# First head's q half-strips stacked two value tiles later, their swaps bound behind value-tile stores in the transfer queue

## Chip, core and metric

The kernel runs on one core of one Trainium2 chip. The metric is the device time of one execution in microseconds (us). The kernel before took 1435.74 us (median of three runs, 1434.72 to 1436.17). The trace is of one profiled execution that took 1434.23 us, of which 1432.4 us lie between the first and the last instruction (the span). All times of day below are in us from the start of that span.

## What is computed

A two-layer encoder trunk on 1024 tokens of width 1024, in f32. Layer 0 is a differential attention, layer 1 a latent attention; only layer 0 matters here, and of it the start:

```python
def _diff_attention(h, positions, w_in, ...):
    proj = h @ w_in
    q, k, v, z = jnp.split(proj, [DA_WIDTH, 2 * DA_WIDTH, 3 * DA_WIDTH], axis=-1)
    q = _rope(q.reshape(b, s, 2 * DA_HEADS, DA_QK_DIM), positions)
    k = _rope(k.reshape(b, s, 2 * DA_HEADS, DA_QK_DIM), positions)
    ...
        sc = jnp.einsum('bqhcd,bkhcd->bhcqk', qb, k, preferred_element_type=f32) * scale
        p = jax.nn.softmax(sc, axis=-1)
        p = p[:, :, 0] - lam * p[:, :, 1]
        return jnp.einsum('bhqk,bkhd->bqhd', p.astype(v.dtype), v)
```

Each of 8 heads has two q and two k vectors of 64 per token (c = 0 and 1) and a value vector of 128. Beside this, every layer has shift, scale and gate vectors, each a product of a 1024-vector with a weight matrix (`_modulation`).

## The kernel before

Every f32 operand of a product is kept as two parts, high (rounded) and low (the rest), and a product is three matmuls (`mm3`, L186, L187, L188). Tokens come in two halves of 512 and in eight tiles of 128.

The engines work from queues that are filled at build time: a scheduler orders each engine's instructions, and an engine takes them strictly in that order. A transfer is issued by SP; an SP instruction that waits holds back every transfer behind it. Each SP transfer signals on one of eight semaphores in turn, and the ninth waits for the first. `tc.issue_after(ins)` adds one rule for the scheduler: what is traced inside the block comes after `ins` on the engine that `ins` is on.

The stretch that the change touches lies between 95 and 170 us, ahead of the attention loop of layer 0:

- **Value tiles.** The loop `for tt in range(8)` (L885) makes the values of heads 4 to 7 for eight token tiles, here called tile 0 to 7. `v0_tile` runs 24 matmuls into one PSUM bank (`vps`); `store_v` copies it out as a high part (ScalarE, L366, `v_hl<-vps`), subtracts for the low part (VectorE, the same line), and SP sends both to a scratch tensor in HBM (L368, `vS<-v_hl`, 512 KB). For tiles 0 to 5 the two-part tile `v_hl` has two buffers (`VB[0] = 2`): tile 2 needs the store of tile 0 to have landed, tile 3 that of tile 1, and so on. Tiles 6 and 7 (`V_LATE = 6`) take theirs from the buffers of the next item.
- **Modulation loads.** `next(mods_g)` loads 512 KB of a modulation weight (L423, `ada<-in_ada_ss` or `ada<-in_ada_g`) and lets VectorE reduce it (L444). The loop runs 13 of these (`MODS`), here called load 1 to 13, on three buffers: load 4 needs the reduction of load 1 to be done, and so on; tile 6 takes the buffer of load 11.
- **The first head's q and k.** Their projections were made before the loop. `rope` copies a half-strip out of PSUM, has SP swap its rows (L330), and multiplies; the closures left over for later are kept in the list `pend`: for each of k half 0, k half 1, q half 0 and q half 1 a rotation (GpSimd, L336) and a stacking. The four of k run before the loop. `stack_q` makes the two-part tiles `qa` and `qb` that the scores read: two ScalarE copies (L356, L357), two GpSimd subtractions (L358, L359), and four SP transfers of 128 KB inside SBUF (L361 and L362, the "swaps"), which copy each part into the other half of the partitions.
- **PSUM banks.** The accumulators of tiles 3 and 4 lie in the two banks that tiles 6 and 7 take again; so the first matmul of tile 6 waits for tile 3 to be copied out.
- **First scores.** At tile 6 the first head's first score tile is traced (`q_tile(0, 0, 0, ...)`, L873); the scheduler puts its matmuls near the end of tile 7. It reads `qa` and `qb` of q half 0. Row maximum (VectorE L404) and exponential (ScalarE L406) follow.

The code that places the stacking:

```python
    pend = [t for t in side.q if t]
    ...
        for t in pend[4 + 2 * tt : 6 + 2 * tt]:
            t()
        v0_tile(tt, 1, wv1)
```

Of the kernel before, what the change touches and what calls it, by code (L numbers as in the profile page):

```python
# [91 lines left out]
def trunk(ctx: ExitStack, tc: tile.TileContext, A, out):  # L92
# [22 lines left out]
    def psum(name, **tags):  # L115

        nonlocal ps, turn
        pst.close()
        NB.clear()
        NB.update(tags)  # L120
        turn = 0
        ps = pool(pst, name, bufs=1, space=PSUM)
# [642 lines left out]
    def v0_tile(tt, fh, wv):  # L765
        half, tl = tt // 4, tt % 4
        acc = bank("acc", "vps")
        c_ = slice(tl * P, (tl + 1) * P)
        for k in range(KT):
            hh, hl = h0[k][half]  # L770
            mm3(acc, hh[:, c_], hl[:, c_], wv[k][0], wv[k][1], k == 0, k == KT - 1)
        if tt < V_LATE:
            store_v(0, p1b, acc, tt, fh)
        else:
            store_v(0, pm, acc, tt, fh, "ada", 3)
# [80 lines left out]
    pend = [t for t in side.q if t]  # L856
# [6 lines left out]
    def q_tile(h, half, ti, zz, ep, mid=lambda i: None):  # L863

        ql = slice(ti * P, (ti + 1) * P)
        zs = [zz[:, ti : ti + 1], sm.tile([P, 1], F32, name="z1")]
        es = []
        qa, qb = QS[h][half]
        for c in range(2):
            s_ps = bank("sc", "s", [P, T])  # L870
            for src, fst in ((qa, True), (qb, False)):
                for kc in range(2):
                    PE.matmul(s_ps[:, kc * HF : (kc + 1) * HF], src[:, c, ql], KS[h][kc][:, c, :], start=fst, stop=not fst)  # L873
            with tc.issue_after(combined[-1]) if c == 0 and combined else nullcontext():
                es.append(softmax_part(None if c else ep, s_ps, zs[c], 1 if ep is a0a else 3))
            mid(c)
        e0, e1 = es
        z0, z1 = zs
        V.reciprocal(z1, z1)
        V.tensor_scalar(z1, z1, z0, neglam[:, 0:1], op0=ALU.mult, op1=ALU.mult)  # L880
        combined.append(V.scalar_tensor_tensor(out=e0, in0=e1, scalar=z1[:, 0:1], in1=e0, op0=ALU.mult, op1=ALU.add).ins)  # L881
        return e0

    first, combined = [], []
    for tt in range(8):  # L885
        if tt == V_LATE:
            psum("ps2", sc=2, tr=1, pv=1)
            zz0 = sm.tile([P, 4], F32, name="zz")
            first += [zz0, q_tile(0, 0, 0, zz0, a0a)]
        for _ in range(MODS[tt]):  # L890
            next(mods_g)
        for t in pend[4 + 2 * tt : 6 + 2 * tt]:
            t()
        v0_tile(tt, 1, wv1)
        if tt == HOLD:
            with tc.issue_after(store_v.last):
                for raw, src in held:
                    SP.dma_start(raw, src)
# [1046 lines left out]
```

## Time and profile before

| | before |
|---|---|
| median of 3 runs | 1435.74 us |
| profiled execution | 1434.23 us |
| its span | 1432.4 us |
| TensorE (PE) busy | 1399.6 us |
| VectorE (DVE) busy | 903.7 us |
| ScalarE (ACT) busy | 743.4 us |
| GpSimd (POOL) busy | 602.7 us |
| HBM and SBUF traffic | 201.64 MB, mean 141 GB/s |

PE is the engine that matters: a microsecond in which PE stands still, or runs at a lower clock, ahead of the attention loop is a microsecond that nothing later is known to hide. The other engines and the transfer queue count only where PE waits for them. "SPq" is SP's own queue: the time at which an instruction is issued there, not when its data lands. "PEclk" in a table of windows is the granted TensorE clock, 1.00 being full.

### The profile page before, as it was taken

What the parts mean: (1) busy time and instruction counts of PE and PEld (TensorE: products, weight loads), DVE (VectorE), ACT (ScalarE), POOL (GpSimd) and SP (SyncE); (2) the same over time, 40 slices, a digit from 0 to 9 for tenths busy, and PEclk for the clock granted to TensorE, in tenths of its full rate; (3) what the DMA queues carried; (4) which work ended last, traced back from release to release, by engine and by line L of the source; (5) the groups of instructions that cost most, each with busy time, mean ns of one, the idle gap of its engine ahead of it and who ended that gap; (6) DMA issues with size and microseconds to landing.
All of it is one profiled execution on the core that took longest, in us unless ns stands there. A gap on an engine that the chain in (4) does not pass through costs nothing.

```text
span 1432.4 us, 20749 instructions
## 1 busy us (share of the span) xinstructions
PE 1399.6 (98%) x7478; PEld 1169.8 (82%) x7478; DVE 903.7 (63%) x1366; ACT 743.4 (52%) x1318; POOL 602.7 (42%) x483
## 2 busy tenths in 40 slices
PE   9998999999999999998999999999999999999997
PEld 7786788888888887887888778887888888888886
DVE  7655687667777767677445877255566555555355
ACT  6622366656565656566443644345455554545442
POOL 4424164656564646453561244413241331412562
PEclk9999899999999999999999999999999999999999
DMA  9876723233333333336663232466343432336663
GB/s 355 263 232 199 242 66 103 82 104 84 99 84 96 88 97 82 104 85 225 216 224 117 61 104 88 140 182 180 110 117 114 132 100 77 103 96 213 218 209 138
DMA packets 128473, 201.64 MB, mean 141 GB/s; under 512 B 17777, under 2 KB 54769, under 8 KB 128370
## 3 DMA queue, kind: packets, MB, share of 16 engines
q1 hardware_dynamic: 128370, 200.31, 45.3%
q8 instruction: 59, 0.97, 0.3%
q14 instruction: 44, 0.36, 0.1%
HBM read 131.11 MB, written 45.55 MB: 123 GB/s over the span
## 4 chain that ended last, share of the span: by engine, by line
PE 84%; DMA 4%; DVE 4%; ACT 2%; POOL 2%; issue 2%; SPq 1%; POOLq 0%; ACTq 0%; DVEq 0%
PE s L1702 10%; PE acc L186 9%; PE acc L188 9%; PE acc L187 9%; PE tr L387 7%; PE s L873 7%; PE pv L187 4%; PE pv L188 4%; PE pv L186 4%; PE oacc L187 3%; PE oacc L188 3%; PE oacc L186 3%; PE zacc L186 1%; PE zacc L188 1%; PE zacc L187 1%
## 5 line engine op out<-in xcount | busy, mean ns | idle before, releaser
L389 ACT CAST pth<-tr 128x512 fp32r<-128x512 f32 x256 | 150.3, 587 | 279.8 <-PE tr L387 276.8
L404 DVE TENSOR_REDUCE nm<-s 128x1 f32<-128x1024 f32 x192 | 233.9, 1219 | 76.5 <-PE s L873 70.1
L390 DVE TENSOR_TENSOR ptl<-tr,pth 128x512 fp32r<-128x512 f32 x256 | 176.1, 688 | 136.6 <-ACT pth L389 136.1
L235 POOL TENSOR_TENSOR wl<-wraw,wh 128x512 fp32r<-128x512 f32 (+2 forms) x82 | 101.4, 1239 | 232.2 <-ACT wh L234 204.7
L387 PE MATMUL tr<-ident,e 128*128 128x128 f32 x1024 | 154.7, 273 | 4.1 <-DVE ptl L390 3.9
L406 ACT ACTIVATE e<-s,nm 128x1024 f32<-128x1024 f32 x128 | 143.5, 1121 | 28.9 <-DVE nm L404 28.5
L387 PEld LDWEIGHTS tr<-ident,e 128*128 128x128 f32 x1024 | 120.8, 140 | 45.9 <-DVE ptl L390 22.5
L186 PE MATMUL acc<-h0h,wh 128*128 128x512 f32 x360 | 151.0, 419 | 1.7 <-DVE v_hl L366 1.7
L186 PE MATMUL pv<-pth,vt 128*128 128x256 f32 x512 | 147.3, 288 | 0.0
L187 PE MATMUL pv<-ptl,vt 128*128 128x256 f32 x512 | 145.8, 285 | 0.0
L188 PE MATMUL pv<-pth,vt 128*128 128x256 f32 x512 | 144.6, 282 | 0.0
L188 PE MATMUL acc<-h0h,wl 128*128 128x512 f32 x360 | 142.9, 397 | 0.0
L187 PE MATMUL acc<-h0l,wh 128*128 128x512 f32 x360 | 142.0, 395 | 0.0
L1117 POOL TENSOR_TENSOR wol<-wor,woh 128x512 fp32r<-128x512 f32 x64 | 85.0, 1348 | 84.2 <-ACT woh L1116 84.0
L186 PEld LDWEIGHTS pv<-pth,vt 128*128 128x128 f32 x512 | 97.3, 190 | 3.2 <-ACT pth L389 0.8
L187 PEld LDWEIGHTS pv<-ptl,vt 128*128 128x128 f32 x512 | 97.4, 190 | 2.8
L188 PEld LDWEIGHTS pv<-pth,vt 128*128 128x128 f32 x512 | 97.7, 191 | 0.1
L873 PE MATMUL s<-ks,qa 128*128 128x512 f32 x256 | 82.8, 404 | 3.5 <-DVE e L881 2.7
L331 POOL TENSOR_TENSOR rp_r<-rp_raw,cosT 128x512 f32<-128x512 f32 x38 | 49.6, 1306 | 85.4 <-ACT rp_raw L326 52.1
L336 POOL TENSOR_TENSOR rp_sw<-rp_sw,sinT 128x512 f32<-128x512 f32 x42 | 55.6, 1324 | 71.1 <-DMA rp_sw<-rp_raw 70.9
L881 DVE SCALAR_TENSOR_TENSOR e<-s,z,e 128x1024 f32<-128x1024 f32 x64 | 82.1, 1283 | 2.1
L873 PE MATMUL s<-ks,qb 128*128 128x512 f32 x256 | 81.0, 396 | 0.4 <-DMA qb<-qb 0.4
(624 smaller groups left out, 3359.4 us busy)
## 6 DMA issues: line engine op xcount, KB each, us to landing
ada<-in_ada_ss SPq DMA_DIRECT2D x32, 512.0 KB, 6.7
wraw<-in_w_s SPq DMA_DIRECT2D x64, 256.0 KB, 2.8
vS<-v_hl SPq DMA_DIRECT2D x32, 512.0 KB, 4.8
vt<-vS SPq DMA_DIRECT2D x32, 512.0 KB, 4.6
wor<-in_w_out SPq DMA_DIRECT2D x64, 256.0 KB, 3.5
rp_sw<-rp_raw SPq DMA_DIRECT2D x168, 64.0 KB, 2.0
bc_s<-bc_d SPq DMA_DIRECT2D x30, 256.0 KB, 4.3
oS<-bc_s SPq DMA_DIRECT2D x30, 256.0 KB, 2.6
```

The lines of the kernel that those rows point to most:

```text
L186: PE.matmul(psum, ah, bh, start=first, stop=False)
L187: PE.matmul(psum, ah, bl, start=False, stop=False)
L188: return PE.matmul(psum, al, bh, start=False, stop=last).ins
L235: sub = (lo_on or (V if pair_of else G)).tensor_sub(l_[:, :n], raw[:, :n], f32v(h_[:, :n]))
L387: PE.transpose(tr[:, j, :], p[:, kt * P : (kt + 1) * P], ident)
L389: mk["S"] = S.copy(pth[kh][:, :, dst], tr).ins
L390: mk["V"] = V.tensor_sub(ptl[kh][:, :, dst], tr, f32v(pth[kh][:, :, dst])).ins
L404: mk["V"] = V.reduce_max(nm, s_ps, axis=AX.X, negate=True).ins
L406: mk["S"] = S.activation(e, s_ps, AF.Exp, bias=nm, scale=1.0, accum_out=zs).ins
L873: PE.matmul(s_ps[:, kc * HF : (kc + 1) * HF], src[:, c, ql], KS[h][kc][:, c, :], start=fst, stop=not fst)
L1117: in_turn(G.tensor_sub(lo, raw, f32v(hi)))
L1702: PE.matmul(s_ps[:, kc * HF : (kc + 1) * HF], lhs, rhs(kc), start=i == 0, stop=i == 4)
```

## The change

```diff
@@ -889,8 +889,9 @@
             first += [zz0, q_tile(0, 0, 0, zz0, a0a)]
         for _ in range(MODS[tt]):
             next(mods_g)
-        for t in pend[4 + 2 * tt : 6 + 2 * tt]:
-            t()
+        for t in pend[2 * tt : 2 + 2 * tt] if tt > 1 else ():
+            with tc.issue_after(store_v.last):
+                t()
         v0_tile(tt, 1, wv1)
         if tt == HOLD:
             with tc.issue_after(store_v.last):
```

q half 0 is now rotated and stacked in the round of tile 2 instead of tile 0, and q half 1 in that of tile 3 instead of tile 1. Whatever these closures issue on SP comes behind the store that was traced last at that point: the store of tile 1 for half 0 and that of tile 2 for half 1. Nothing is added or removed. All lines of the file from L894 on move down by one.

On SP, before, from the store of tile 0 (first row; `vS_1_70` is the scratch tensor of heads 4 to 7) to the store of tile 1 (last row):

```order
L368 DMA vS_1_70<-v_hl 256x4x128
L361 DMA qa<-qa 64x512
L362 DMA qa<-qa 64x512
L361 DMA qb<-qb 64x512
L362 DMA qb<-qb 64x512
L423 DMA ada<-in_ada_ss 128x1024 x2
L361 DMA qa<-qa 64x512
L362 DMA qa<-qa 64x512
L361 DMA qb<-qb 64x512
L362 DMA qb<-qb 64x512
L368 DMA vS_1_70<-v_hl 256x4x128
```

All eight swaps stand between the two stores, and loads 3 and 4 between the two sets of swaps. On SP, now, from the store of tile 0 to the store of tile 2:

```order
L368 DMA vS_1_70<-v_hl 256x4x128
L423 DMA ada<-in_ada_ss 128x1024 x2
L368 DMA vS_1_70<-v_hl 256x4x128
L423 DMA ada<-in_ada_ss 128x1024
L423 DMA ada<-in_ada_g 128x1024
L361 DMA qa<-qa 64x512
L362 DMA qa<-qa 64x512
L361 DMA qb<-qb 64x512
L362 DMA qb<-qb 64x512
L368 DMA vS_1_70<-v_hl 256x4x128
```

Only loads 3 and 4 are left between the stores of tiles 0 and 1; the swaps of half 0 stand behind loads 5 and 6 and ahead of the store of tile 2. Then follow, now:

```order
L423 DMA ada<-in_ada_g 128x1024 x2
L361 DMA qa<-qa 64x512
L362 DMA qa<-qa 64x512
L361 DMA qb<-qb 64x512
L362 DMA qb<-qb 64x512
L368 DMA vS_1_70<-v_hl 256x4x128
L423 DMA ada<-in_ada_g 128x1024 x3
```

The swaps of half 1 stand behind loads 7 and 8 and ahead of the store of tile 3; from there on SP's order is as it was.

On PE one matmul of tile 7 changes sides with the first score tile. This piece of the difference is at the end of tile 7 (`vps` is the tile's accumulator, `s` the scores):

```order
 L186 MATMUL vps<-wvh,h0h_1_128 128x512
-L873 MATMUL s<-ks,qa 128x512 x2
-L873 MATMUL s<-ks,qb 128x512 x2
-L873 MATMUL s<-ks,qa 128x512 x2
-L873 MATMUL s<-ks,qb 128x512 x2
 L187 MATMUL vps<-wvl,h0h_1_128 128x512
+L873 MATMUL s<-ks,qa 128x512 x2
+L873 MATMUL s<-ks,qb 128x512 x2
+L873 MATMUL s<-ks,qa 128x512 x2
+L873 MATMUL s<-ks,qb 128x512 x2
 L188 MATMUL vps<-wvh,h0l_1_129 128x512
```

The scores come one matmul later. The orders of VectorE, ScalarE and GpSimd are the same before and now.

## The prediction

> **What bounds the kernel now.** I began with the page: busy times, and the chain that ended last.
>
> ```profile
> PE 1399.6 (98%) x7478; PEld 1169.8 (82%) x7478; DVE 903.7 (63%) x1366; ACT 743.4 (52%) x1318; POOL 602.7 (42%) x483
> PE 84%; DMA 4%; DVE 4%; ACT 2%; POOL 2%; issue 2%; SPq 1%; POOLq 0%; ACTq 0%; DVEq 0%
> ```
>
> PE sets the end, so a change of transfer order is worth what PE stands still or runs slowly for it. I therefore asked for the waits between 95 and 175 us (total, count, longest):
>
> ```profile
> ACT v_hl L366 <- DMA vS<-v_hl: 20.5, 2, 16.5
> PE vps L186 <- DVE v_hl L366: 5.3, 1, 5.3
> PE acc L186 <- DVE v_hl L366: 1.7, 1, 1.7
> ```
>
> One PE wait of 5.3 us stands in a value tile, and one ScalarE wait of 16.5 us for a store. PE's timeline shows what it costs (start, duration, bracket: idle before):
>
> ```profile
> 135.83 0.39 PE L188 MATMUL vps<-wvh,h0l 128*128 128x512 f32 x1
> 141.49 0.79 PE L186 MATMUL vps<-wvh,h0h 128*128 128x512 f32 x1 [5.27 <-DVE v_hl L366]
> 142.09 0.63 PE L187 MATMUL vps<-wvl,h0h 128*128 128x512 f32 x1
> ...
> 146.35 0.63 PE L188 MATMUL vps<-wvh,h0l 128*128 128x512 f32 x1
> ...
> 147.14 0.39 PE L187 MATMUL vps<-wvl,h0h 128*128 128x512 f32 x1
> ...
> 153.49 0.39 PE L188 MATMUL vps<-wvh,h0l 128*128 128x512 f32 x1
> 153.72 0.39 PE L186 MATMUL vps<-wvh,h0h 128*128 128x512 f32 x1
> 153.95 0.62 PE L873 MATMUL s<-ks,qa 128*128 128x512 f32 x2
> ```
>
> Tile 6 starts at 141.49. At the full step (147.14 to 153.72 in 29 steps, 0.227 us) it would have started at 136.06, so the stall is 5.43 us. Then matmuls step at 0.426 us (142.09 to 146.35 in ten steps) until 146.8. From 141.49 to the first scores at 153.95 stand 43 matmuls, 12.46 us where 43 x 0.227 = 9.76 would do: 2.70 us more. Stall and slow clock are **8.13 us**.
>
> Why PE waited is in the queues of ScalarE and VectorE, which copy tile 3 out:
>
> ```profile
> 140.13 0.58 ACT L366 CAST v_hl<-vps 128x512 fp32r<-128x512 f32 x1 [16.49 <-DMA vS<-v_hl]
> 140.75 0.69 DVE L366 TENSOR_TENSOR v_hl<-vps,v_hl 128x512 fp32r<-128x512 f32 x1 [2.24 <-ACT v_hl L366]
> ```
>
> The copy waits 16.49 us for a store to land. SP's own queue (start and duration of the issue) says which:
>
> ```profile
> 112.13 0.66 SPq L368 DMA_DIRECT2D vS<-v_hl  x1
> 120.60 0.53 SPq L361 DMA_DIRECT2D qa<-qa  x1
> ...
> 129.98 0.46 SPq L362 DMA_DIRECT2D qb<-qb  x1
> 130.53 1.02 SPq L423 DMA_DIRECT2D ada<-in_ada_ss  x2
> 131.65 0.47 SPq L361 DMA_DIRECT2D qa<-qa  x1
> ...
> 134.08 0.73 SPq L368 DMA_DIRECT2D vS<-v_hl  x1
> ...
> 143.11 0.59 SPq L368 DMA_DIRECT2D vS<-v_hl  x1
> ```
>
> The copy of tile 3 needs the buffer of tile 1, whose store SP issues at 134.08, behind eight swaps and loads 3 and 4. The swaps wait for their own operands on GpSimd; meanwhile the transfer engines carry next to nothing (windows: PE, PEld, DVE, ACT, POOL busy, granted clock, DMA share, GB/s):
>
> ```profile
> 120.00:130.00 10.00, 10.00 (x46) 8.26 (x45) 7.25 (x9) 3.54 (x7) 9.72 (x6) 1.00 0.18 41
> 132.00:156.00 24.00, 18.73 (x71) 14.95 (x70) 11.98 (x19) 1.76 (x3) 0.67 (x1) 0.86 1.01 325
> 136.00:138.00 2.00, 0.22 (x1) 0.00 (x0) 0.85 (x3) 0.00 (x0) 0.00 (x0) 1.00 1.07 253
> 141.49:146.78 5.29, 5.29 (x13) 4.13 (x13) 4.24 (x7) 0.58 (x1) 0.00 (x0) 0.50 1.06 343
> 160.50:164.50 4.00, 4.00 (x11) 3.18 (x12) 4.00 (x8) 1.17 (x3) 0.00 (x0) 0.57 0.86 282
> ```
>
> 41 GB/s over ten microseconds, then 325 GB/s for 24: the load is pushed together.
>
> **The change, part by part.** Nothing is computed more or less; PE, VectorE, ScalarE and GpSimd keep their instructions, and all but PE their order. The terms:
>
> *Store of tile 1.* Behind load 4 now, which takes load 1's buffer (VectorE's timeline; the first row is the last reduction of the loads before these 13):
>
> ```profile
> 111.22 1.28 DVE L444 CUSTOM_DVE_ANT_0 ada<-ada,c,vec 128x1024 f32<-128x1024 f32 x1
> ...
> 114.51 0.69 DVE L366 TENSOR_TENSOR v_hl<-vps,v_hl 128x512 fp32r<-128x512 f32 x1 [2.00 <-ACT v_hl L366]
> ...
> 122.87 2.33 DVE L444 CUSTOM_DVE_ANT_0 ada<-ada,c,vec 128x1024 f32<-128x1024 f32 x1
> ...
> 127.36 0.68 DVE L366 TENSOR_TENSOR v_hl<-vps,v_hl 128x512 fp32r<-128x512 f32 x1
> ```
>
> and the time from issue to landing of all 32 stores:
>
> ```profile
> DMA to landing us min/median/max: 3.5/4.8/7.6
> ```
>
> Tile 1's data is ready at 115.20. Load 1's reduction ends at 125.20, so load 4 goes out there and the store at about 125.8 (0.5 us per issue, half of the 1.02 row). By the row's ends it lands between 129.3 and 133.4. Copy, subtraction and PE's start took 141.49 - 140.13 = 1.36 us, so tile 3 is out by 134.8 at the worst, ahead of 136.06. Neither end of the landing costs anything: the 5.43 us go, and I let the 2.70 go with them, since PE then has no idle time ahead of tile 6.
>
> *Store of tile 2, swaps of half 0.* The low parts come from GpSimd:
>
> ```profile
> 128.66 1.29 POOL L359 TENSOR_TENSOR qb<-rp_r,qa 64x512 fp32r<-64x512 f32 x1
> 131.38 1.29 POOL L359 TENSOR_TENSOR qb<-rp_r,qa 64x512 fp32r<-64x512 f32 x1
> ```
>
> Half 0 is ready at 129.95. Loads 5 and 6 ahead of it wait for the reductions of loads 2 and 3, about 127.4 and 129.3 (tile 2's subtraction ends at 128.04, one reduction more). Four swaps take 134.08 - 131.65 = 2.43 us of SP, so the store goes out at about 132.4 and lands by 140.0; tile 4 is out by 141.4, and tile 7 wants its bank at 136.06 + 24 x 0.227 = 141.51. Just in time at the worst end. The swaps are out by 132.4 too, 13 us before the scores read them.
>
> *Store of tile 3, swaps of half 1.* Ready on GpSimd at 132.67; load 8 ahead waits for load 5's reduction, about 134 (it follows tile 3's subtraction and its own landing). Store 3 goes out at about 136.6 instead of 143.11.
>
> *One matmul ahead of the scores.* They begin at 136.06 + 44 x 0.227 = 146.05, which is **7.90 us** earlier; the matmul itself costs PE nothing, but the chain that follows runs through the scores, so 8.13 - 0.23 counts.
>
> *What is late next.* Behind the scores comes VectorE, in an order that stays:
>
> ```profile
> 150.00 1.28 DVE L444 CUSTOM_DVE_ANT_0 ada<-ada,c,vec 128x1024 f32<-128x1024 f32 x1
> 155.07 1.23 DVE L404 TENSOR_REDUCE nm<-s 128x1 f32<-128x1024 f32 x1 [3.78 <-PE s L873]
> ...
> 157.41 1.28 DVE L444 CUSTOM_DVE_ANT_0 ada<-ada,c,vec 128x1024 f32<-128x1024 f32 x1
> ...
> 159.75 0.69 DVE L366 TENSOR_TENSOR v_hl<-vps,v_hl 128x512 fp32r<-128x512 f32 x1
> ```
>
> The first maximum stands behind load 9's reduction (150.00), load 11's (157.41) ahead of the copy of tile 6, for which PE waits 1.7 us. All this should move 7.90 us up, to a maximum at 147.17 and load 11's reduction at 149.51, if the transfers keep up. Loads 4 to 11, stores 1 to 3 and eight swaps are 8 x 0.524 + 3 x 0.524 + 8 x 0.131 = 6.81 MB. At 325 GB/s these are 21.0 us; counted from 126.6 (load 4's issue and an estimated 1.4 us until data flows, as from 130.53 to the crowded window's 132.00) they end at 147.6, 1.9 us early. At 253 GB/s, the thinnest crowded window, they take 26.9 us and end at 153.5, 4.0 us late. So this term costs 0 to 4.0; I take 0.6, close to the 24 us row, for holes where a load waits for a reduction or for one of the eight semaphores (a third of one load's 0.524 MB / 325 GB/s = 1.6 us).
>
> **Sum:** 7.90 - 0.6 = 7.3 us. Against the profiled execution, 1434.23, this gives 1426.9; that execution lay 1.51 us below the median, so for the median **1428.4 us**. A measurement of this kernel tells about 0.2%, 2.9 us, from no change.
>
> *A rule weighed.* The row 141.49:146.78 shows a granted clock of 0.50 for 5.29 us after the stall. The Trainium skill ("TensorE: Matmul & The Clock Gate", Part 1) says that PE falls to half rate after an idle window of about 3.4 us and comes back after some 3.4 us of work; by it the slow stretch would be worth an estimated 1.7 instead of 2.70 us (3.4 us at half rate), and the forecast 6.3. The trace shows longer, and the trace decides.
>
> **Rivals.** *The second slow stretch goes as well.* After the 1.7 us wait at `acc` the clock is 0.57 until 164.5: 4.00 x (1 - 0.57) = 1.7 us. For it: nearly the same wait elsewhere costs no clock if PE's idle time happens to be spread. Against: the chain that makes the wait stays. Then 9.0 us, 1426.7. By the same part of the skill's page an idle time this short should leave the clock alone; the row 160.50:164.50 disagrees.
>
> *Transfers bind.* Below 6.81 MB / (149.51 - 126.6) = 297 GB/s load 11 is late and its lateness is PE's. At 253 GB/s the gain is 3.9 us, 1431.8. For it: share 1.01 over 24 us. Against: bytes that waited now use the empty stretch.
>
> *The change doesn't free the store.* Load 3, which I let go right behind the store of tile 0, was never seen free: SP stood in the swaps. If its buffer, or load 4's, is held to about 134, store 1 leaves as late as before: 1435.7. Against: VectorE is through with the older loads at 111.22 + 1.28 = 112.5, and load 1's reduction stands at 122.87 whatever SP does.
>
> *Slower: the store of tile 3 is now the held one.* It stands behind the four swaps of half 1 and loads 7 and 8. The first maximum cannot start before its landing plus copy 0.62, subtraction 0.69 and load 9's reduction 1.28. If it lands after 155.07 - 2.6 = 152.5, everything behind is later than before; 3 us past that give 1438.7. For it: the same kind of wait held store 1 for 19 us. Against: its operands are on GpSimd by 132.67, 15 us earlier than needed.
>
> **Chances.** Forecast 0.56, second slow stretch gone 0.12, transfers bind 0.14, store not freed 0.11, slower 0.07. Faster by over 0.2%: 0.82; within: 0.11; slower: 0.07. The range takes in the first three: from 1426.7 less the runs' spread downwards, 1425.4, to 1431.8 and half a microsecond of spread, 1432.6.
>
> **What would show it.** Right: store 1 issued near 126, no PE wait ahead of tile 6, clock 1.00 from 120 to 148, first scores near 146, the 41 GB/s stretch filled from 125 on. Wrong: a wait of ScalarE's copy for a store beyond 136, of VectorE's maximum for load 9, or PE's wait at `acc` well over 1.7 us; and a gain at 146 that later stages lose again.

## The result, and the profile after

| | before | with the change |
|---|---|---|
| median, first comparison (6 runs each) | 1436.34 us | 1431.15 us, ratio 0.9963 [0.9950, 0.9976] |
| median, second comparison (25 and 6 runs) | 1433.66 us | 1428.06 us, ratio 0.9959 [0.9945, 0.9974] |
| profiled execution (its span) | 1434.23 (1432.4) us | 1429.47 (1427.7) us |
| PE busy | 1399.6 us | 1396.7 us |

The change makes the kernel faster, by 5.2 and 5.6 us in the two comparisons; 7.3 us were forecast. Both intervals lie wholly below 0.998, so this is more than the 0.2% that a measurement of this kernel can mistake.

The page of the kernel with the change, the busy times and the chain that ended last:

```profile
PE 1396.7 (98%) x7478; PEld 1167.8 (82%) x7478; DVE 903.3 (63%) x1366; ACT 743.3 (52%) x1318; POOL 603.7 (42%) x483
PE 80%; DVE 6%; DMA 5%; issue 3%; ACT 3%; POOL 2%; SPq 1%; ACTq 0%; POOLq 0%; DVEq 0%
```

PE has as many instructions as before and 2.9 us less of busy time (matmuls at a lower clock count as longer). That this is near the 2.70 us of the slow stretch that is gone is partly chance: in a second trace of each kernel, 1398.8 and 1398.6 us, PE's busy time differs by 0.2 us only; the step from 6.3 us to the medians, below, gives part of the reason. PE still sets the end.

The waits between 95 and 175 us, the three rows that answer to those shown of before:

```profile
ACT v_hl L366 <- DMA vS<-v_hl: 21.3, 3, 8.8
...
PE s L873 <- ACT e L406: 2.1, 1, 2.1
PE acc L186 <- DVE v_hl L366: 1.7, 1, 1.7
```

The row of 5.3 us, PE's wait ahead of tile 6, is gone. ScalarE waits for stores as long as before in sum, but in three pieces of at most 8.8 us instead of two of up to 16.5, and none of these pieces reaches PE's value tiles. PE's wait for the exponential of the first scores has grown from 0.5 to 2.1 us; it is taken up below, at what is late next.

SP's own queue (start and duration of the issue):

```profile
114.05 0.66 SPq L368 DMA_DIRECT2D vS<-v_hl  x1
114.81 13.21 SPq L423 DMA_DIRECT2D ada<-in_ada_ss  x2
128.11 0.64 SPq L368 DMA_DIRECT2D vS<-v_hl  x1
...
135.31 0.63 SPq L368 DMA_DIRECT2D vS<-v_hl  x1
136.03 2.28 SPq L423 DMA_DIRECT2D ada<-in_ada_g  x2
138.96 0.47 SPq L361 DMA_DIRECT2D qa<-qa  x1
...
141.46 0.63 SPq L368 DMA_DIRECT2D vS<-v_hl  x1
142.19 5.37 SPq L423 DMA_DIRECT2D ada<-in_ada_g  x3
```

Only loads 3 and 4 stand between the stores of tiles 0 and 1. ScalarE's copies of tiles 1, 3 and 5 (bracket: idle before, and for what):

```profile
116.35 0.59 ACT L366 CAST v_hl<-vps 128x512 fp32r<-128x512 f32 x1 [7.33 <-PE vps L188]
...
134.86 0.58 ACT L366 CAST v_hl<-vps 128x512 fp32r<-128x512 f32 x1 [8.76 <-DMA vS<-v_hl]
...
148.60 0.59 ACT L366 CAST v_hl<-vps 128x512 fp32r<-128x512 f32 x1 [5.90 <-DMA vS<-v_hl]
```

**How to compare two traces here.** The copy of tile 1 lies ahead of everything that the change moves, and yet it starts at 113.89 us in the trace of before and at 116.35 in this one, at 114.72 in a second trace of the changed kernel and at 115.46 in a second trace of the kernel before. What lies ahead of it varies by more than some terms of the sum. So the times of day below are also given from the start of that copy, written "T1 + ...". Store 1 goes out at T1 + 20.2 before (134.08 - 113.89) and at T1 + 11.76 now (128.11 - 116.35). In two traces of each kernel, four points on the path (`acc` is a projection behind the first scores, `pv` the first product with the values):

| trace | T1 | first scores | first maximum | first `acc` matmul | first `pv` matmul |
|---|---|---|---|---|---|
| before | 113.89 | T1 + 40.06 | T1 + 41.18 | T1 + 46.61 | T1 + 65.36 |
| before, second trace | 115.46 | 39.65 | 40.77 | 46.19 | 64.82 |
| with the change | 116.35 | 32.19 | 34.77 | 40.18 | 58.91 |
| with the change, second trace | 114.72 | 32.18 | 34.57 | 39.98 | 59.85 |

On the means, the scores start 7.7 us earlier (39.86 to 32.19), the first row maximum 6.3 (40.98 to 34.67), the first matmul of `acc` 6.3 (46.40 to 40.08), the first product with the values 5.7 (65.09 to 59.38). So 1.4 us are lost between the scores and the maximum. PE's rows show where they appear:

```profile
148.54 0.62 PE L873 MATMUL s<-ks,qa 128*128 128x512 f32 x2
...
153.63 0.72 PE L873 MATMUL s<-ks,qa 128*128 128x512 f32 x2 [2.15 <-ACT e L406]
...
156.53 0.75 PE L186 MATMUL acc<-h0h,wh 128*128 128x512 f32 x1 [1.73 <-DVE v_hl L366]
```

and VectorE's rows between them why:

```profile
149.22 0.69 DVE L366 TENSOR_TENSOR v_hl<-vps,v_hl 128x512 fp32r<-128x512 f32 x1 [2.02 <-ACT v_hl L366]
149.90 1.28 DVE L444 CUSTOM_DVE_ANT_0 ada<-ada,c,vec 128x1024 f32<-128x1024 f32 x1
...
151.12 1.22 DVE L404 TENSOR_REDUCE nm<-s 128x1 f32<-128x1024 f32 x1
```

The scores start at 148.54, the maximum over them at 151.12, 2.58 us later (1.12 before). VectorE goes without a break from tile 5's subtraction to load 9's reduction to the maximum, and the subtraction waits for tile 5's copy, which waits for store 3 to land. The value tiles no longer wait for a store; the maximum now does.

Windows of the changed kernel (PE, PEld, DVE, ACT, POOL busy, granted clock, DMA share, GB/s):

```profile
122.00:132.00 10.00, 9.93 (x44) 8.19 (x45) 9.22 (x11) 4.00 (x8) 9.73 (x6) 1.00 0.37 103
134.00:151.50 17.50, 17.48 (x77) 14.09 (x75) 9.85 (x17) 1.76 (x3) 2.79 (x2) 1.00 1.02 311
156.50:162.00 5.50, 5.47 (x17) 4.39 (x18) 5.48 (x9) 1.20 (x3) 0.00 (x0) 0.69 0.84 272
```

The clock is full up to the scores. After the two waits it is 0.69 for 5.50 us in this trace, a loss of 5.50 x 0.31 = 1.7 us, the same as before; in the second trace of the changed kernel it is lower and costs more (below). And the transfers are as crowded as before: 1.02 of the engines' time at 311 GB/s.

### The profile page after: what moved, and what is told of

It reads as the page before. It is cut to its first block, busy times and chain, and to the rows that moved or that the text cites. A ratio compares the mean times of both kernels' runs of the same rounds, so it can differ in the third digit from the quotient of the medians.

```text
span 1427.7 us, 20748 instructions
## 1 busy us (share of the span) xinstructions
PE 1396.7 (98%) x7478; PEld 1167.8 (82%) x7478; DVE 903.3 (63%) x1366; ACT 743.3 (52%) x1318; POOL 603.7 (42%) x483
## 3 DMA queue, kind: packets, MB, share of 16 engines
HBM read 131.11 MB, written 45.55 MB: 124 GB/s over the span
## 4 chain that ended last, share of the span: by engine, by line
PE 80%; DVE 6%; DMA 5%; issue 3%; ACT 3%; POOL 2%; SPq 1%; ACTq 0%; POOLq 0%; DVEq 0%
PE s L1703 9%; PE acc L188 8%; PE acc L186 8%; PE acc L187 8%; PE tr L387 7%; PE s L873 7%; PE oacc L186 4%; PE oacc L188 4%; PE oacc L187 4%; PE pv L187 4%; PE pv L188 4%; PE pv L186 4%; DVE ada L444 2%; PE zacc L186 1%; PE zacc L188 1%
## 5 line engine op out<-in xcount | busy, mean ns | idle before, releaser
L390 DVE TENSOR_TENSOR ptl<-tr,pth 128x512 fp32r<-128x512 f32 x256 | 176.1, 688 | 136.6 <-ACT pth L389 136.1
```

What stands on the lines that cost most here:

```text
L390: mk["V"] = V.tensor_sub(ptl[kh][:, :, dst], tr, f32v(pth[kh][:, :, dst])).ins
```

## The experiments

Every kernel computes the whole reference. Three theories are named by letters in what was expected. **Q**, the queue: what counts is only the order on SP, that is, when stores 1 and 2 go out. **P**, the place of the arithmetic: what counts is where the rotation and stacking stand in the program, and what the scheduler makes of it. **D**, the transfers: behind the scores the engines that carry the data are full, and what is left to gain goes with the bytes ahead of store 3. Ratios are against runs of the kernel before on the same chip, with their 95% intervals.

**The change again** (`after_again`), no edit.

> Theory Q (queue): the gain is that SP lets the store of tile 1 out about 8 us earlier; what is missing of the forecast 7.3 us is a later store of tile 3 (1.5 us where 0.6 was forecast) and chance ahead of the change. Then the profile shows the copy of tile 1 to the store of tile 1 in about 11.8 us, first scores 32.2 us behind the copy of tile 1, and the time is 5.0 to 7.0 us below before. If the 2.5 us by which the copy of tile 1 stood later in the first profile (116.35 instead of 113.89) are chance, it stands near 114 to 115 now; if they belong to this build, near 116.3 again. Rival D (transfers bind): the gain is what the transfer engines allow, under 4 us.

Measured: 1428.06 against 1433.66 us, 0.9959 [0.9945, 0.9974]. Its trace has store 1 at T1 + 11.76, to the hundredth as in the first; no wait ahead of tile 6; the maximum 2.39 us behind the scores. The gain and the loss behind the scores are both properties of the kernel; T1, at 114.72 instead of 116.35, is not.

**Only the swaps moved** (`swaps_only`). In the kernel before, rotation and stacking stay in rounds 0 and 1; only the swaps are kept back, and traced behind the stores of tiles 1 and 2.

```diff
-        for t in (qa, qb):
-            SP.dma_start(f32v(t[64:128, 0, :]), f32v(t[0:64, 0, :]))
-            SP.dma_start(f32v(t[0:64, 1, :]), f32v(t[64:128, 1, :]))
+        def swap():
+            for t in (qa, qb):
+                SP.dma_start(f32v(t[64:128, 0, :]), f32v(t[0:64, 0, :]))
+                SP.dma_start(f32v(t[0:64, 1, :]), f32v(t[64:128, 1, :]))
...
+        if tt in (1, 2):
+            with tc.issue_after(store_v.last):
+                held_swaps.pop(0)()
```

> The stacking is traced where it was before; only the eight swaps are taken out of it and issued behind the stores of tile 1 (half 0) and tile 2 (half 1). Theory Q (SP's order is all of the change): the stores of tile 1 goes out 11.8 us behind the copy of tile 1, PE has no wait ahead of tile 6, and from the copy of tile 1 to the first matmul at acc it takes 40 to 41 us (before 46.6, the change 40.2 and 40.0); the time is that of the change within 1 us. Rival P (the place of the stacking's arithmetic matters): the gain is clearly smaller than the change's, 3 us or less.

SP's queue of this kernel (its lines are numbered 8 higher, so that the stores are L376 and the loads L431):

```profile
114.08 12.69 SPq L431 DMA_DIRECT2D ada<-in_ada_ss  x2
126.87 0.64 SPq L376 DMA_DIRECT2D vS<-v_hl  x1
...
133.72 0.64 SPq L376 DMA_DIRECT2D vS<-v_hl  x1
```

T1 is 115.09, so store 1 leaves at T1 + 11.78, as with the change. Measured: 1428.53 against 1434.02 us, 0.9964 [0.9950, 0.9977]; `acc` starts at T1 + 40.81. This is the change's gain without moving a line of the arithmetic. Q holds, P falls.

**Only half 1 moved** (`half1_only`). Half 0 stays in the round of tile 0, half 1 goes to that of tile 3.

```diff
-        for t in pend[2 * tt : 2 + 2 * tt] if tt > 1 else ():
-            with tc.issue_after(store_v.last):
+        for t in {0: pend[4:6], 3: pend[6:8]}.get(tt, ()):
+            with tc.issue_after(store_v.last) if tt > 1 else nullcontext():
```

> Half 0's stacking and swaps as before, half 1's as in the change. The store of tile 1 then stands behind four swaps (last operand ready 16.1 us behind the copy of tile 1) and loads 3 and 4: it goes out about 17.7 us behind that copy (before 20.2, the change 11.8). Theory Q: tile 3 comes out some 2.2 us earlier than before, PE's wait ahead of tile 6 shrinks from 5.3 to 3 or 3.5 us and does not vanish; from the copy of tile 1 to acc about 44 us with the slow clock still behind the wait, 42 without; time 2 to 4.5 us below before. Rival D (transfers bind): the gain does not follow the store of tile 1, and is as large as the change's or none.

SP's queue and, below it, PE at the start of tile 6:

```profile
131.41 0.46 SPq L362 DMA_DIRECT2D qb<-qb  x1
131.96 1.02 SPq L423 DMA_DIRECT2D ada<-in_ada_ss  x2
133.04 0.64 SPq L368 DMA_DIRECT2D vS<-v_hl  x1
```

```profile
140.90 0.80 PE L186 MATMUL vps<-wvh,h0h 128*128 128x512 f32 x1 [3.23 <-DVE v_hl L366]
```

With four swaps still ahead of it, store 1 leaves at T1 + 17.71 (T1 is 115.33) and PE waits 3.23 us, with the slow clock behind it (0.52 in the window from 141 to 147). Measured: 1431.57 against 1434.02 us, 0.9982 [0.9971, 0.9992]; `acc` at T1 + 44.99. Store 1 is 2.5 us earlier than before, PE's wait 2.0 us shorter, `acc` 1.4 earlier, and the time 2.5 us less. The stall follows the store's issue; but of the 6.3 us at `acc` only these 1.4 come without the swaps of half 0.

**A third buffer instead, before and after** (`vb3_before`, `vb3_after`): `v_hl` of tiles 0 to 5 gets three buffers, so that tile 3 needs the store of tile 0, which went out long before, instead of that of tile 1.

```diff
-VB = (2, 5)
+VB = (3, 5)
```

> The kernel before with a third buffer for the value tiles of layer 0; SP keeps its order, so the store of tile 1 still goes out behind all swaps, near 134. Theory Q: PE's 5.3 us wait was for the buffer alone, so it is gone here too: tile 6 starts without a wait, first scores near 146, and the time is 4 to 7 us below before, less than without crowding since loads 9 to 11 still go out late. Rival D: with SP's order unchanged the loads arrive as late as before; the wait moves from PE ahead of tile 6 to the row maximum behind load 9, and the gain is under 3 us.

> The change with a third buffer for the value tiles of layer 0. Tile 5 then needs the store of tile 2, not that of tile 3. Theory Q: what the change still loses between the scores and the first row maximum (1.5 us) sits in the store of tile 3, so it goes: 1.0 to 1.5 us less than the change. Rival D: load 9 lands just behind, and under 0.5 us is won.

Measured: 1430.49 against 1433.66 us, 0.9976 [0.9965, 0.9987], for the kernel before with it, and 1429.30 against the same, 0.9969 [0.9957, 0.9980], for the changed kernel with it. ScalarE's copy of tile 3 and PE's scores in the former:

```profile
125.53 0.59 ACT L366 CAST v_hl<-vps 128x512 fp32r<-128x512 f32 x1 [1.76 <-PE vps L188]
```

```profile
142.24 0.64 PE L873 MATMUL s<-ks,qa 128*128 128x512 f32 x2
...
154.72 1.19 PE L873 MATMUL s<-ks,qa 128*128 128x512 f32 x2 [4.14 <-DVE e L881]
```

Tile 3 is copied as soon as PE has made it, at 125.53 instead of 140.13, and PE has no wait ahead of tile 6, although store 1 goes out at 134.24, as late as before: so it was the store's hold on the buffer that stopped PE. But the scheduler now puts the first scores earlier, at 142.24, and PE waits 4.14 us a little later for VectorE. The experiment shows the cause of the stall; its time, 3.2 us below before where theory Q had 4 to 7, isn't that of the stall alone. With the change and a third buffer PE waits 5.2 us at `acc` (1.7 with the change alone), and nothing is gained, where theory Q had 1.0 to 1.5 us.

**Half 1 another tile later** (`half1_tile4`): half 1 in the round of tile 4, behind store 3, so that store 3 has no swaps of half 1 ahead of it.

```diff
-        for t in pend[2 * tt : 2 + 2 * tt] if tt > 1 else ():
+        for t in {2: pend[4:6], 4: pend[6:8]}.get(tt, ()):
```

> The stacking of q half 1 goes to the round of tile 4, behind the store of tile 3; half 0 as in the change. Theory Q: the store of tile 3 goes out about 3 us earlier, behind loads 7 and 8 alone (22 instead of 25.1 us behind the copy of tile 1), the copy of tile 5 follows, and the first row maximum stands right behind the scores: 1.0 to 1.5 us less than the change, 6.0 to 8.5 less than before. Rival D: the swaps only change places with the store, load 9 or 11 lands as late as now, and the time is that of the change within 0.5 us.

Measured: 1429.37 against 1433.66 us, 0.9968 [0.9958, 0.9978]: not better than the change. Store 3 leaves at T1 + 21.6 instead of T1 + 25.1, but the scheduler again draws the scores forward (T1 + 28.99) and PE waits 4.3 us for VectorE. A miss: the order of PE changed with it, so it says nothing clean of store 3.

**Two loads behind store 1 instead of ahead of it** (`loads_a`). Store 1 follows store 0 at once, and the loads of round 1 go to round 2.

```diff
-MODS = (2, 2, 2, 2, 3, 2, 0, 0)
+MODS = (2, 0, 4, 2, 3, 2, 0, 0)
...
-            next(mods_g)
+            with tc.issue_after(store_v.last) if tt > 1 else nullcontext():
+                next(mods_g)
```

> The change, with loads 3 and 4 traced two tiles later, so that the store of tile 1 stands directly behind that of tile 0. Theory Q: that store goes out about 4 us behind the copy of tile 1; tile 3's copy no longer waits for it, load 5 is reduced earlier, load 8 and with it the store of tile 3 go out 1.5 to 3 us earlier, and the first row maximum stands right behind the scores: copy of tile 1 to acc 38.7 to 39.2 us, 1.0 to 1.5 us below the change. Rival D: loads 9 to 11 land as late as in the change, and the time is that of the change within 0.5 us.

SP's queue, then ScalarE's copy of tile 5:

```profile
113.32 3.75 SPq L368 DMA_DIRECT2D vS<-v_hl  x2
117.11 11.90 SPq L423 DMA_DIRECT2D ada<-in_ada_ss  x3
...
139.61 0.63 SPq L368 DMA_DIRECT2D vS<-v_hl  x1
```

```profile
147.23 0.59 ACT L366 CAST v_hl<-vps 128x512 fp32r<-128x512 f32 x1 [6.74 <-DMA vS<-v_hl]
```

Both stores leave in the first row, the second about 10 us earlier than with the change. T1 is 115.10. Store 3 leaves at T1 + 24.5, 0.6 to 0.8 earlier than with the change, yet tile 5's copy starts at T1 + 32.13 (32.25 and 32.04 with the change), and `acc` at T1 + 40.03 (40.18, 39.98). Measured: 1428.67 against 1434.02 us, 0.9963 [0.9950, 0.9976], the change's ratio. Beyond the change's order, an earlier store 1 is worth nothing: Q ends there.

**The kernel before again** (`before_again`), one execution, for a second trace.

> The kernel before once more, for its trace. If where the copy of tile 1 stands (113.89 before, 116.35 and 114.72 in two traces of the change) is chance, it falls anywhere in 113 to 117; from there to acc it takes 46.6 us within 0.4 us, with the 5.3 us wait ahead of tile 6.

Measured: 1434.48 us; the wait ahead of tile 6 is 5.2 us again, `acc` at T1 + 46.19.

**One more load** (`extra_load`): to the changed kernel, 512 KB that nobody reads are loaded behind load 8, ahead of the swaps of half 1 and of store 3.

```diff
+        if tt == 3:
+            for i in range(1):
+                with tc.issue_after(store_v.last):
+                    SP.dma_start(p1b.tile([P, 2, HF], F32, name="extra", tag="extra", bufs=1), A["ada_g0"][i].rearrange("p (a b) -> p a b", a=2))
```

> The change plus one transfer of 512 KB that nobody reads, issued between load 8 and the swaps of half 1. The engines' orders stay, but for the first scores, which stand 4 matmuls (0.9 us) later on PE. Theory D (behind the scores the transfer engines bind): load 9 lands later by what 0.524 MB take at 302 to 325 GB/s, 1.6 to 1.7 us, and the first row maximum, 34.6 and 34.8 us behind the copy of tile 1 in the two traces of the change, stands at 36.0 to 36.6; acc at 41.3 to 41.9 (change 40.0 and 40.2); time 1.2 to 2 us above the change, 4 to 5 below before. Theory Q (SP's order and waits bind): only the 0.4 us of one more issue, acc within 0.5 us of the change.

VectorE's rows of this kernel behind the scores (which start at 149.42):

```profile
150.82 0.69 DVE L366 TENSOR_TENSOR v_hl<-vps,v_hl 128x512 fp32r<-128x512 f32 x1 [4.43 <-ACT v_hl L366]
151.52 1.28 DVE L444 CUSTOM_DVE_ANT_0 ada<-ada,c,vec 128x1024 f32<-128x1024 f32 x1
152.73 1.22 DVE L404 TENSOR_REDUCE nm<-s 128x1 f32<-128x1024 f32 x1
```

T1 is 116.36. In PE's order the scores stand four matmuls later; the maximum doesn't wait for them. Store 3 leaves at T1 + 25.70 (T1 + 25.11 and 25.28 with the change) and takes 8.15 us to tile 5's copy at 150.21, where it took 6.8 to 7.1; the maximum starts at T1 + 36.37, 1.6 to 1.8 us later, and `acc` at T1 + 41.78, also 1.6 to 1.8 later. One load's bytes at the crowded window's rate are 0.524 MB / 311 GB/s = 1.7 us. The maximum moves by the bytes: on the path D holds. Measured: 1430.73 against 1433.01 us, 0.9983 [0.9974, 0.9992]. That is 2.3 us below before where D had 4 to 5, so the time lost 1.1 to 1.7 us more than `acc` did, and why stays open.

**Fewer loads ahead of store 3** (`mods1`, `mods4`): the same 13 loads, four of them moved to the last two rounds, so that seven and six instead of eight are ahead of store 3.

```diff
-MODS = (2, 2, 2, 2, 3, 2, 0, 0)
+MODS = (2, 2, 2, 1, 1, 1, 2, 2)
```

for `mods1`, and (2, 2, 1, 1, 1, 2, 2, 2) for `mods4`.

> The change with the gate loads spread out, MODS = (2, 2, 2, 1, 1, 1, 2, 2): one load instead of two ahead of tile 3's store, so that two loads fewer (1.05 MB) stand ahead of the first row maximum; the scores are placed some matmuls earlier. Theory D: the first maximum stands within 1.3 us of the scores (change 2.4 and 2.6), and acc comes 1 to 2.5 us earlier than in the change, 37.5 to 39 us behind the copy of tile 1; time 1 to 2.5 us below the change. Theory Q: acc as in the change, within 0.5 us, since the store of tile 3 still waits behind the swaps of half 1.

> As the run beside it, spread further: MODS = (2, 2, 1, 1, 1, 2, 2, 2). Three to four loads fewer ahead of the first maximum. Theory D: no more is to be had than the 1.3 us between maximum and scores; acc 37.5 to 39 us behind the copy of tile 1, time 1 to 2.5 us below the change. If the loads that now come behind the scores collide with the first head's value loads, PE waits for those in the first pass of the attention loop and 1 to 3 us are lost again.

Measured: 1427.38 and 1426.56 against 1433.01 us, 0.9964 [0.9950, 0.9978] and 0.9956 [0.9944, 0.9969]. PE in `mods4`, and the windows up to 160 us:

```profile
153.75 0.70 PE L873 MATMUL s<-ks,qa 128*128 128x512 f32 x2 [2.35 <-DVE e L881]
...
155.39 0.50 PE L186 MATMUL acc<-h0h,wh 128*128 128x512 f32 x1
```

```profile
130.00:150.00 20.00, 20.00 (x90) 16.50 (x89) 12.28 (x17) 3.36 (x6) 5.65 (x4) 1.00 1.07 325
150.00:160.00 10.00, 7.62 (x35) 5.82 (x34) 9.44 (x16) 3.11 (x6) 0.00 (x0) 1.00 0.71 220
```

Here store 3 leaves at T1 + 22.57 (137.93, with T1 at 115.36), the scheduler puts the scores at T1 + 28.99 and four more of their matmuls ahead of `acc`, PE waits 2.35 us instead of 2.15 and 1.73, and the clock stays at 1.00. The first `pv` comes at T1 + 57.86 (57.27 in `mods1`), 1.0 and 2.0 us earlier than in the two traces of the change. The first maximum is earlier too, at T1 + 31.79 (T1 + 32.89 in `mods1`, 34.77 and 34.57 with the change); but the scores are as well, and it still starts 2.33 us behind them in `mods1` and 2.80 in `mods4`. Theory D had the maximum within 1.3 us of the scores in `mods1`, and `acc` at T1 + 37.5 to 39 in both; `acc` came at T1 + 40.1 and 40.0. These are misses, and the two kernels don't separate the bytes from the place of the scores. Both beat the kernel before; that either beats the change is not shown, since the intervals overlap nearly whole.

## Why the prediction was right, and where it was not

- **What bounded the kernel** was read rightly: store 1, held on SP by swaps that waited for GpSimd, kept a buffer, the copy of tile 3 waited for it, and PE for the copy. A third buffer took the wait away with the store as late as ever; moving the swaps alone gave the whole gain; moving half of them gave a smaller part.
- **Store 1 and tile 3.** Forecast: issued at 125.8, which is T1 + 11.9; measured T1 + 11.76 twice. It was to land between T1 + 15.4 and T1 + 19.5; the copy of tile 3, which waits for it, starts at T1 + 18.5 and 17.4, and PE doesn't wait. The 5.43 us went, and the 2.70 us of slow clock with them.
- **Store 2 and the swaps of half 0.** Forecast 132.4, T1 + 18.5; measured T1 + 18.96 (135.31). PE doesn't wait at tile 7. Right.
- **The first scores**, 7.90 us earlier by the forecast, came 7.7 earlier on the means. Right.
- **Store 3** was to go out at 136.6, T1 + 22.7. It went out at T1 + 25.11 and 25.28: 2.4 to 2.6 us late. The row of loads 7 and 8 (2.28 us of issue) stands ahead of it, and load 8 waits for load 5's reduction, which comes after tile 3's subtraction; then SP waits another 0.6 us (1.3 in the second trace) for a load to land, and the swaps of half 1 begin only at 138.96. It then took 6.8 to 7.1 us until the copy of tile 5 could start, near the 7.6 at the upper end of the forecast's row.
- **What is late next** is the term that was mis-sized. It put 0.6 us, from bounds of 0 and 4.0, for transfers that hold the work behind the scores; the runs show 1.3 to 1.5. The wait was named as one to look for (the maximum behind load 9's reduction), but the sum counted the bytes only up to load 11, at 325 GB/s, the rate of the fuller stretch of before. What decided was store 3's landing in the middle of that stretch, at 311 GB/s. The prediction has this chain too, under the rival "slower": store 3's landing, then 2.6 us for copy, subtraction and load 9's reduction (2.52 and 2.53 measured). With store 3 out at T1 + 22.7 and the slowest landing, 7.6 us, it gave the maximum at T1 + 32.9, just ahead of the forecast T1 + 33.3, so it cost nothing; with the issue as measured it gives 25.1 + 7.1 + 2.5 = T1 + 34.8 and 25.3 + 6.8 + 2.5 = T1 + 34.6, the two maxima of the table. An earlier issue alone doesn't help: in `loads_a` store 3 left 0.6 to 0.8 us earlier and landed no earlier, after 7.6 us. One load more put 1.6 to 1.8 us on the maximum, as many as its bytes take. So the transfers that were held back behind the empty stretch were only partly brought into it: the profile of the changed kernel, in 40 slices of the time from 112 to 150 us, still shows an empty stretch while SP waits to issue load 4:

```profile
GB/s 73 61 82 232 364 364 418 373 363 419 220 4 0 0 0 0 0 86 246 298 339 354 294 107 265 319 177 223 331 356 416 418 265 200 272 361 382 412 367 310
```

  A slice is 0.95 us; from the twelfth on, 122.5 us, almost nothing moves for six slices. The prediction wanted this stretch filled from 125 on (T1 + 11); it is filled from 128.2 (T1 + 11.8), so in its own time the step is right, and the bytes were still too many for what came after.
- **The wait at `acc` and the slow clock behind it** stayed, as forecast: 1.7 us and, in the first trace, 1.7 us. The rival in which this stretch goes as well did not come about with this change; in `mods1` and `mods4` it does, with the clock at 1.00.
- **From 6.3 us at `acc` to 5.2 and 5.6 us in the medians.** On the means 0.6 us are lost between `acc` and the first `pv`. All of it is in one trace: from `acc` to `pv` it takes 18.75 and 18.63 us in the traces of before and 18.73 in the first of the change, but 19.87 in the second, where the slow clock lasts longer: the first 13 matmuls of `acc` take 5.71 us (154.70 to 160.41) where 13 x 0.227 = 2.95 would do, 2.8 us more. A window of that trace:

```profile
156.00:160.00 4.00, 4.00 (x11) 3.03 (x11) 3.65 (x6) 0.52 (x1) 0.00 (x0) 0.50 0.64 215
```

  So with the same waits ahead of it (1.95 and 1.72 us against 2.15 and 1.73) the slow stretch has no fixed price, and 1.1 of the 1.9 us by which PE's busy time differs between the two traces of the change are these. From the first `pv` to the end of the span the four traces take 1252.4 to 1253.2 us, 1252.8 on the means of both kernels: no later stage loses what was gained. The forecast sum of 7.3 was thus too large by 0.7 to 0.9 for the mis-sized term and, where the slow clock lasts longer, by 1.1 more (2.8 instead of 1.7). The traces' 5.7 us at `pv` and the medians' 5.2 and 5.6 differ by less than T1 varies.
- **The range.** Its ends don't come out of their own terms: 1426.7 less the 1.02 us by which the lowest run lay below the median is 1425.7, not 1425.4, and 1431.8 plus half a microsecond is 1432.3, not 1432.6. The measured 1431.15 lies inside either way.

**The clock.** With 3.23 us of idle PE the clock in `half1_only` falls to 0.52 for 6 us, and after 0.47 and 1.71 us in the kernel before to 0.57, while a single wait of 2.35 us in `mods4`, and 0.30 and 1.86 us in `mods1`, leave it at 1.00. The Trainium skill ("TensorE: Matmul & The Clock Gate", Part 1) puts the fall after an idle window of some 3.4 us, and calls the window free-running. The shorter waits here that cost clock disagree with the length; that waits of like length fare differently would fit a window that starts at its own times, but no run here varied only that.

## What to carry to other kernels

Where one queue issues all transfers, look at what stands ahead of a store whose buffer somebody needs: a few small transfers that wait for a slow engine can hold it for longer than everything they carry takes, and moving only these, not the work that feeds them, gave the whole gain here. When such a wait goes, the next one is found by following the same kind of transfer (here the store two tiles later) through the crowded stretch, not by comparing the total of the bytes with its end. And compare traces from the last common event ahead of the change: here the time of that event alone varied by 3.5 us between traces.

## What was not expected of the hardware

- The stretch ahead of the change varies: the copy of tile 1 started between 113.89 and 116.35 us in the four traces of the two kernels, and up to 117.38 in the others.
- VectorE's reduction (L444), 1.28 us in most rows, took 2.33 us at 122.87 in the kernel before, and 1.79 us at 136.15 in the changed kernel, where load 8 and store 3 wait behind it:

```profile
136.15 1.79 DVE L444 CUSTOM_DVE_ANT_0 ada<-ada,c,vec 128x1024 f32<-128x1024 f32 x1
```

  GpSimd's subtraction (L359), 1.29 us at 128.66 in the kernel before, when VectorE had just gone idle, took 2.15 us a little earlier (at 131.11), beside another long reduction. That the two engines slow each other is likely from these rows, but no run took one of them away.
- One and the same store of 512 KB took 6.8 to 7.1 us from its issue to the copy that waits for it, and 8.15 with one load more ahead of it in the queue.
